# Half of the weight remainders of a two-block transformer: a DMA that adds, in place of GpSimd's subtract

## The chip, the cores and the metric

The kernel runs on one core of one Trainium2 chip, as one launch. The metric is the device time of the launch in microseconds (us), lower is better.

## What is computed

A residual stream of 512 tokens with 1024 features, all in float32, goes through two blocks.

```
def first_block(x, ...):
    for layer in range(2):
        u = rmsnorm(h, norm_mix[layer])
        mix = hgrn2_mixer(u, ...) if layer == 0 else dilated_attention_mixer(u, ...)
        h = h + mix
        h = h + swiglu_ffn(rmsnorm(h, norm_ffn[layer]), ffn_w_in[layer], ffn_w_down[layer])
    return rmsnorm(h, final_norm)

def second_block(x, ...):
    proj = rmsnorm_2(x, norm_mix) @ w_in
    ...
    x = x + (gate_a * (o_a @ w_up_nsa) + gate_b * (o_b @ w_up_gla)) @ w_out
    x = x + (silu(h @ w_ffn_gate) * (h @ w_ffn_up)) @ w_ffn_down
    return rmsnorm_2(x, norm_final)
```

HGRN2 is a linear attention with a forget factor for each feature (8 heads of 128). The dilated attention has 12 heads of 128 in three groups. In the second block `o_a` is a native sparse attention (8 heads of 64 with a compressed, a selected and a window branch) and `o_b` a gated linear attention (4 heads). The feed-forwards have 2816 hidden features. Nearly all of the arithmetic is in products of the 512 tokens with weight matrices.

## The kernel before

**Products.** TensorE (PE) reads operands of the type float32r. Each operand x is split into a head, x cast to float32r, and a remainder (rest), x minus head. `mm3` (line 387) makes a product of three matmuls: rest by head, head by head, head by rest. A feature-major product takes 128 weight columns at a time: one weight block of 128 x 128 against 512 tokens is three matmuls.

**Weights.** `Weights` (line 240) streams the weights in the order of use. The blocks of a section (`hgrn`, the feed-forwards, `attn`, `blk2`) are packed into units of up to 1024 columns, 512 KB; there are 346 units, numbered u = 0 to 345. The first eight are of 512 columns. A unit goes three ways:

- `load`: SP issues the DMA from HBM into `w_raw` (three buffers).
- `heads`: ScalarE (ACT) casts `w_raw` to the head `w_hi`.
- `rests`: VectorE (DVE) for even u, GpSimd (POOL) for odd u, subtracts `w_hi` from `w_raw` into `w_lo`. A pair of `w_hi` and `w_lo` is a split block; there are three.

`take` hands the blocks of a unit to PE, and calls the others as it goes:

```
        if self.idx == 3 * len(widths) // 8:
            self.heads(self.look)
        if self.idx == 5 * len(widths) // 8:
            self.rests()
```

So after 3/8 of unit `at` the heads up to unit `at + look - 1` are put on ACT's queue, after 5/8 the rests on DVE's and GpSimd's. `look` is 1 at first and becomes `SPLIT` in `hgrn` when x[5] has been split (line 807). A unit of a feed-forward is 8 blocks, 24 matmuls.

**Order.** Each engine runs its instructions in the order in which the program lays them out. The mixers are generators, whose steps the program puts between weight products (`tick`, `step`). When a step comes is decided by `Clock` (line 163), a rough model of the four engines with a cost for each instruction issued through the wrappers `v`, `a`, `g` and `t`; a step waits until its inputs should be there. DMAs are no part of that model. The steps' instructions, such as the queries `Q` of HGRN's blocks, `GQ` and `GK` of the gated linear attention, `Pc` of the compressed branch and `P` of attention, are mostly on DVE, and PE then multiplies what they wrote. GpSimd makes, beside the rests, products such as `Q`, `KT`, `T`, `rot`, `rs`, `sg` and the sums of squares `sq_acc`.

At the start the first value products of HGRN take one x tile at a time (`first`, line 802): ACT makes the head of u of x[k], then its square, with the heads of the weights between them, and PE multiplies x[k] with unit k, 12 matmuls.

Nearly every row of the profile has the line L228, that of the recording helper; tiles tell the instructions apart.

Of the kernel before, what the change touches and what calls it, by code (L numbers as in the profile page):

```python
# [22 lines left out]
UNIT = 1024  # L23

# columns of the packed per-feature vectors
# [10 lines left out]
# columns of the constants that stay  # L36
# [9 lines left out]
# the pairs of heads before which HGRN's value products for heads 0..3 and 4..7 come  # L46
HGRN_V = {0: 0, 2: 1}
# attention's sections: the queries and keys of a head of each group, the values of a group's heads
# [4 lines left out]
def nsa_rows():  # L53
    """Feature order of the NSA heads: tile j holds head j of group 0 and head j of group 1."""
    return np.concatenate([np.arange((e * 4 + j) * 64, (e * 4 + j) * 64 + 64) for j in range(4) for e in range(2)])


def attn_heads():
    """(head of the group, group) in the order in which the output projection takes them."""
    return [(t, g) for t in range(4) for g in (1, 2)] + [(t, 0) for t in range(4)]  # L60


def weight_plan():
    """The order in which weight blocks are used: (section, [(matrix, k tile, columns)])."""
# [74 lines left out]
def plan_units(sec, chunks):  # L139
    """Cut a section's blocks into units of at most UNIT columns; the first ones are small, to start early."""  # L140
    units, cur, w = [], [], 0
    for i, ch in enumerate(chunks):
        n = len(ch[2])
        if w + n > UNIT or (sec == "hgrn" and w and i <= KD):
            units.append((cur, w))
            cur, w = [], 0
        cur.append(ch)
        w += n
    if cur:
        units.append((cur, w))  # L150
    return units
# [11 lines left out]
class Clock:  # L163
    """Rough times of the engines' queues and of the tiles' contents while the program is laid out:
    they say when a background step's inputs and banks will be there, so that TensorE isn't made to wait."""

    def __init__(self, hop):
        self.hop = hop  # from an instruction's end to the start of another engine's that waits for it
        self.free = {"pe": 0.0, "v": 0.0, "a": 0.0, "g": 0.0}
        self.written, self.read = {}, {}  # L170
        self.held = []
# [4 lines left out]
    def banks(self, now):  # L176
        """PSUM banks that are free by then."""
        def free(x):
            r, w = self.read.get(x, (-1.0, "")), self.written.get(x, (0.0, ""))
            return w[0] <= r[0] <= now - self.hop  # L180
        self.held = [x for x in self.held if not free(x)]
        return 8 - len(self.held)
# [57 lines left out]
class Weights:  # L240
    """Streams the weights in the order of use and splits each into its float32r head and rest."""

    RAW, SPLIT = 3, 3
# [18 lines left out]
    def heads(self, look):  # L262
        while self.n_head < min(self.at + look, len(self.units)):
# [5 lines left out]
            self.a.copy(hi[:, :w], self.raw[u][:, :w])  # L269
            self.split[u] = (hi, lo)  # L270
            self.n_head += 1

    def rests(self):
        while self.n_rest < self.n_head:
            u = self.n_rest
            w = self.units[u][2]
            hi, lo = self.split[u]
            (self.g if u % 2 else self.v).tensor_sub(lo[:, :w], self.raw.pop(u)[:, :w], hi[:, :w].bitcast(F32))
            self.n_rest += 1
        self.load(self.n_rest + self.RAW - 1)  # L280
# [31 lines left out]
class Program:  # L312
# [74 lines left out]
    def mm3(self, out, a, b, first, last):  # L387
        """out += a^T b for operands given as (head, rest)."""
# [18 lines left out]
    def gemm(self, xs, M, evac, lead=1, ms=None):  # L407
        """Feature-major product: evac(m, [128 features, 512 tokens]) for each output tile m.
        An operand may be a pair of functions: whether it is there, and what makes it."""
# [13 lines left out]
    def gemm_tok(self, n, residue=False, before=None, after=None, every=1):  # L423
        """Token-major product with n weight columns: four banks of 128 tokens, by blocks or by the rest of the token mod 4."""
# [24 lines left out]
    def norm_feed(self, k, squares=True):  # L449
        """x[k] is final: build the operand's parts and add its squares."""  # L450
# [25 lines left out]
    def sums(self, out, acc, residue=False):  # L476
        """Each token's sum over the partitions of acc, onto the token's partition."""
# [33 lines left out]
    def bcast(self, col, ps=None):  # L511
        """[128 tokens, n] to the first 128 n columns of a PSUM bank that hold every token's value on all partitions."""
# [50 lines left out]
    #  # L563
    # A head's score of query t and key s <= t is q_t . (forget factors of s+1..t) k_s. Keys and queries meet
    # block by block: when neighbouring blocks of h tokens are joined, the queries carry the factors from their
    # block's start, the keys those to their block's end and T holds each block's product, so that every factor
    # is a product of forget factors and nothing is divided.
# [5 lines left out]
    def decay4(self, Q, K, T, have, Vj, done):  # L573
        """Two heads whose values are there when have() says so, with keys K[e] [128, 512] and forget
        factors T [128, 2, 512]; Q[e] [128, 2, 512] holds head e's queries and,
        beside them, room. Blocks are joined four at a time: the room takes the queries that reach back further
        than the block before theirs, with the factors of the blocks between.
        Vj(e, j) gives head e's values of tokens 128 j.. as [tokens, 128]; done(e, o) takes the normed output,
        not yet times its gain."""
        v, a, g = self.v, self.a, self.g  # L580
        # per level: each block's product, and the products of the blocks after each of the first three
# [25 lines left out]
        def begin(e, h, T):  # L607
            """The room's queries for blocks of h tokens."""
# [57 lines left out]
    def decay2(self, Q, K, T, Vj, done):  # L666
        """Two heads on one set of keys K and forget factors T [128, 1, 512], whose queries Q [128, 2, 512] are
        zero outside each head's features. Blocks are joined two at a time."""
# [39 lines left out]
    def decay_out(self, Q, K, T, Sd, have, Vj, done):  # L708
        """Sd holds the scores within each block of 128 tokens. The blocks before come through a state
        [features, values] that is carried from block to block."""  # L710
# [49 lines left out]
    def hgrn(self):  # L760
# [16 lines left out]
        # TensorE's clock is released by activity: these run while the first operands are on their way  # L777
# [99 lines left out]
    def attn(self):  # L877
# [13 lines left out]
        def scores(gi, q, k, st):  # L891
            """Masked scores and their exponentials of one head, four blocks of 128 queries."""
# [27 lines left out]
        def merge(hg, st):  # L920
            """Softmax over the three groups' log-sum-exps, then the weighted outputs."""
# [109 lines left out]
    def block2(self):  # L1031
# [28 lines left out]
        # compressed keys and values  # L1060
# [30 lines left out]
        # gated linear attention operands  # L1091
# [25 lines left out]
        # token-major columns  # L1117
# [62 lines left out]
        # sparse attention  # L1180
# [4 lines left out]
        def rope(raw, i):  # L1185
            """Rotate, then stack the parts of the 64 features for products in two passes: q as head on one
            half of the partitions and rest on the other, k's head on both halves and k's rest on both."""
# [92 lines left out]
        def w_stage(j, e, br, P, l):  # L1280
            """Softmax's sum and the branch's gate, onto the rows of P."""
# [5 lines left out]
        def pt_stage(P):  # L1287
            """P transposed to keys x queries, in parts: [(key block, head, rest)] with columns of queries from there on."""
# [16 lines left out]
        def pv_stage(j, e, br, PT):  # L1305
            """Value products; the values' heads go to rows 0..63 and their rests to rows 64..127."""
# [150 lines left out]
    def finish(self, hh):  # L1457
        """The last output tile in two halves of the tokens, so that the first half is normed and stored under the second."""
# [29 lines left out]
        def store(p, factors, k):  # L1488
            """Feature tiles k and k + 1."""
# [68 lines left out]
def levels():  # L1558
    """Where a key (row) and a query (column) meet as blocks are joined: two at a time, for blocks of 1..32 tokens
    and the second blocks' queries; then four at a time, for blocks of 1, 4 and 16, with the queries of the last  # L1560
    three blocks against the block before theirs, of the last two against the first and of the last against the second."""
# [11 lines left out]
def rope_tables():  # L1573
    """cos, and the sine with the sign that the other half takes; both [128 dims, 512 tokens]."""
# [6 lines left out]
def rope2_tables():  # L1581
    """Tables of the partial rotation for two stacked heads of 64, and the swap of its two halves."""
# [12 lines left out]
def feat(a):  # L1595
    """A vector over features as [128, tiles]."""
    return np.asarray(a, np.float32).reshape(-1, 128).T
# [54 lines left out]
```

## Time and profile before

| what | value |
|---|---|
| median of 3 runs | 2163.91 us (2163.86 to 2165.43) |
| span of the profiled execution, first to last instruction | 2162.1 us |
| difference of the two | 1.8 us |
| matmuls | 9983 |
| granted clock of PE, mean | 0.994 |
| HBM read | 187.25 MB |

The profiled execution is known by its span; its time as a run is not given apart, so 1.8 us beside the span stand for what lies around it. A row of a timeline gives the start and the length in us, the engine, the operation with output and inputs, and in brackets for how long the engine stood idle before it and what released it. PE is the matmul side of TensorE, PEld its weight loads.

### The profile page before, as it was taken

What the parts mean: (1) busy time and instruction counts of PE and PEld (TensorE: products, weight loads), DVE (VectorE), ACT (ScalarE), POOL (GpSimd) and SP (SyncE); (2) the same over time, 40 slices, a digit from 0 to 9 for tenths busy, and PEclk for the clock granted to TensorE, in tenths of its full rate; (3) what the DMA queues carried; (4) which work ended last, traced back from release to release, by engine and by line L of the source; (5) the groups of instructions that cost most, each with busy time, mean ns of one, the idle gap of its engine ahead of it and who ended that gap; (6) DMA issues with size and microseconds to landing.
All of it is one profiled execution on the core that took longest, in us unless ns stands there. A gap on an engine that the chain in (4) does not pass through costs nothing.

```text
span 2162.1 us, 25412 instructions
## 1 busy us (share of the span) xinstructions
PE 2117.4 (98%) x9983; PEld 1773.4 (82%) x9983; DVE 1004.3 (46%) x1775; ACT 783.8 (36%) x1290; POOL 723.6 (33%) x442
## 2 busy tenths in 40 slices
PE   9999999999999999999999999999899999999998
PEld 7787788888888998788888888887688788888887
DVE  4778853322334555643322333447778753222322
ACT  5343443222233433443222224244455543222233
POOL 4413343323333434323322335331511253322333
PEclk9999999999999999999999999999999999999999
DMA  5111233323323222222332232321111223333332
GB/s 178 59 59 49 69 127 98 98 98 98 98 88 107 79 88 78 79 69 98 98 102 93 98 98 92 133 69 48 55 55 57 70 95 98 98 98 98 96 100 69
DMA packets 55865, 191.00 MB, mean 88 GB/s; under 512 B 6257, under 2 KB 8321, under 8 KB 55745
## 3 DMA queue, kind: packets, MB, share of 16 engines
q1 hardware_dynamic: 53584, 183.85, 26.2%
q0 software_dynamic: 1008, 3.42, 0.4%
q10 hardware_dynamic: 1152, 2.10, 0.3%
q8 instruction: 78, 1.28, 0.2%
q14 instruction: 43, 0.34, 0.1%
HBM read 187.25 MB, written 2.10 MB: 88 GB/s over the span
## 4 chain that ended last, share of the span: by engine, by line
PE 86%; DVE 9%; issue 1%; POOL 1%; ACT 1%; DMA 1%; SPq 0%; DVEq 0%; ACTq 0%; POOLq 0%
PE ps L228 86%; DVE Q L228 2%; DVE Sd L228 2%; DVE P L228 1%; DMA w_raw<-in_hgrn 1%; DVE w_lo L228 1%; DVE K L228 0%; POOL rot L228 0%; DVE Pc L228 0%; DVE qs L228 0%; POOL rs L228 0%; DVE obl L228 0%; DVE GQ L228 0%; DVE PT L228 0%; POOL w_lo L228 0%
## 5 line engine op out<-in xcount | busy, mean ns | idle before, releaser
L228 PE MATMUL ps<-u,w_hi 128*128 128x512 f32 x3392 | 1049.4, 391 | 0.0
L228 PEld LDWEIGHTS ps<-u,w_hi 128*128 128x128 f32 x3392 | 638.9, 188 | 128.9 <-issue 1.4
L228 PE MATMUL ps<-u,w_lo 128*128 128x512 f32 x1696 | 683.7, 403 | 2.2 <-POOL w_lo L228 2.2
L228 POOL TENSOR_TENSOR w_lo<-w_raw,w_hi 128x1024 fp32r<-128x1024 f32 (+2 forms) x173 | 415.8, 2403 | 745.1 <-ACT w_hi L228 636.2
L228 ACT CAST w_hi<-w_raw 128x1024 fp32r<-128x1024 f32 (+2 forms) x346 | 356.1, 1030 | 301.6 <-PE ps L228 205.4
L228 PEld LDWEIGHTS ps<-u,w_lo 128*128 128x128 f32 x1696 | 319.7, 189 | 68.3 <-issue 4.2
L228 PE MATMUL ps<-h,w_hi 128*128 128x512 f32 (+1 forms) x1078 | 326.3, 385 | 0.0
L228 DVE TENSOR_TENSOR w_lo<-w_raw,w_hi 128x1024 fp32r<-128x1024 f32 (+2 forms) x173 | 231.5, 1338 | 183.7 <-ACT w_hi L228 175.4
L228 PEld LDWEIGHTS ps<-h,w_hi 128*128 128x128 f32 x1078 | 200.9, 188 | 40.4
L228 PE MATMUL ps<-h,w_lo 128*128 128x512 f32 (+1 forms) x539 | 207.6, 385 | 0.5 <-DVE x L228 0.5
L228 POOL TENSOR_TENSOR sg<-sg,r_bc 128x512 f32<-128x512 f32 x66 | 85.8, 1299 | 290.3 <-ACT sg L228 290.3
L228 DVE TENSOR_TENSOR x<-x,ps 128x512 f32<-128x512 f32 (+1 forms) x73 | 49.5, 678 | 218.6 <-PE ps L228 218.6
L228 PE MATMUL ps<-w_hi,u 128*128 128x512 f32 (+1 forms) x448 | 139.1, 392 | 2.3 <-DVE u L228 2.3
L228 DVE TENSOR_TENSOR h<-ps,sg 128x512 f32<-128x512 f32 x66 | 45.7, 692 | 194.9 <-PE ps L228 182.4
L228 ACT ACTIVATE sg<-gs 128x512 f32<-128x512 f32 x66 | 41.7, 632 | 242.3 <-DVE gs L228 242.3
L228 ACT CAST h<-h 128x512 fp32r<-128x512 f32 x66 | 41.0, 620 | 242.8 <-DVE h L228 242.8
L228 DVE TENSOR_TENSOR gs<-ps,r_bc 128x512 f32<-128x512 f32 x66 | 45.6, 691 | 156.8 <-PE ps L228 156.7
L228 PEld LDWEIGHTS ps<-h,w_lo 128*128 128x128 f32 x539 | 101.2, 188 | 20.9 <-DVE x L228 0.7
L228 ACT ACTIVATE P<-P,nm 128x128 f32<-128x128 f32 (+2 forms) x112 | 55.2, 494 | 142.6 <-DVE nm L228 130.4
L228 POOL TENSOR_TENSOR sq_acc<-sq_acc,sq 128x512 f32<-128x512 f32 x48 | 67.2, 1405 | 117.8 <-ACT sq L228 115.7
L228 PEld LDWEIGHTS ps<-w_hi,u 128*128 128x128 f32 x448 | 95.0, 226 | 10.3 <-DVE u L228 2.7
L228 PE MATMUL ps<-w_lo,u 128*128 128x512 f32 (+1 forms) x224 | 85.8, 383 | 0.0
(294 smaller groups left out, 2231.5 us busy)
## 6 DMA issues: line engine op xcount, KB each, us to landing
w_raw<-in_ffn SPq DMA_DIRECT2D x198, 512.0 KB, 3.5
w_raw<-in_attn SPq DMA_DIRECT2D x48, 512.0 KB, 3.5
w_raw<-in_blk SPq DMA_DIRECT2D x47, 512.0 KB, 3.4
w_raw<-in_hgrn SPq DMA_DIRECT2D x36, 512.0 KB, 3.5
w_raw<-in_blk SPq DMA_DIRECT2D x7, 404.0 KB, 2.9
x<-in_xt SPq DMA_DIRECT2D x8, 256.0 KB, 5.1
w_raw<-in_hgrn SPq DMA_DIRECT2D x8, 256.0 KB, 4.0
x<-in_xt ACTq DMA_DIRECT2D x8, 256.0 KB, 5.0
```

Source lines behind the costliest of these rows:

```text
L228: r = f(*args, **kw)
```

## The change

From unit 9 on, an odd unit's remainder is no longer a subtract on GpSimd. ACT writes the head, as before, and then the negative of the head into `w_lo`. GpSimd then issues a DMA that reads the weights from HBM a second time and adds them to what stands in `w_lo`. Even units keep their subtract on DVE, and units 1, 3, 5 and 7 theirs on GpSimd. Four split blocks are held instead of three, and with them `look` becomes 4. The scratch space for GpSimd's DMA descriptors, `dynamic_dma_scratch_size`, is set to 4096. Comments and docstrings are left out as well, which the diff below doesn't show.

```diff
-    RAW, SPLIT = 3, 3
+    RAW, SPLIT, DIRECT = 3, 4, 8
...
             self.a.copy(hi[:, :w], self.raw[u][:, :w])
+            if u >= self.DIRECT and u % 2:
+                self.a.activation(lo[:, :w], hi[:, :w].bitcast(F32), AF.Copy, scale=-1.0)
             self.split[u] = (hi, lo)
...
-            w = self.units[u][2]
+            ap, _, w = self.units[u]
             hi, lo = self.split[u]
-            (self.g if u % 2 else self.v).tensor_sub(lo[:, :w], self.raw.pop(u)[:, :w], hi[:, :w].bitcast(F32))
+            raw = self.raw.pop(u)
+            if u < self.DIRECT or u % 2 == 0:
+                (self.g if u % 2 else self.v).tensor_sub(lo[:, :w], raw[:, :w], hi[:, :w].bitcast(F32))
+            else:
+                self.nc.gpsimd.dma_start(lo[:, :w], ap, accum_op=ALU.add)
...
-    nc = bacc.Bacc("TRN2", target_bir_lowering=False, num_devices=1)
+    nc = bacc.Bacc("TRN2", target_bir_lowering=False, num_devices=1, dynamic_dma_scratch_size=4096)
```

The first place is ACT's queue at the start of the program. `x_96`, `x_98` and `x_100` are x[5], x[6] and x[7]; the two casts of 128x512 are units 6 and 7, the casts of 128x1024 units 8, 9 and, in the second fence, 10. Before:

```order
L228 CAST w_hi_258<-w_raw_232 128x512
L228 CAST w_hi_261<-w_raw_256 128x512
L228 ACTIVATE sq_270<-x_96 128x512
L228 ACTIVATE u_285<-x_98,vec_78 128x512
L228 CAST w_hi_288<-w_raw_266 128x1024
L228 ACTIVATE sq_294<-x_98 128x512
L228 ACTIVATE u_309<-x_100,vec_78 128x512
```

After the change:

```order
L228 CAST w_hi_258<-w_raw_232 128x512
L228 CAST w_hi_261<-w_raw_256 128x512
L228 CAST w_hi_266<-w_raw_264 128x1024
L228 ACTIVATE sq_276<-x_96 128x512
L228 ACTIVATE u_291<-x_98,vec_78 128x512
L228 CAST w_hi_294<-w_raw_272 128x1024
L228 ACTIVATE w_lo_295<-w_hi_294 128x1024
L228 ACTIVATE sq_301<-x_98 128x512
L228 ACTIVATE u_316<-x_100,vec_78 128x512
```

The cast of unit 8 has moved ahead of the square of x[5] and of u of x[6], the cast of unit 9 ahead of u of x[7], with the new negation behind it.

The second place is GpSimd's queue in block 2, where the gated linear attention begins and the rotations (`rot`) of the sparse attention's keys and queries stand. Before:

```order
L228 TENSOR_TENSOR rot<-kraw,tab 128x512
L228 TENSOR_TENSOR rot<-rot,rot_10466 128x512
L228 TENSOR_TENSOR w_lo<-w_raw,w_hi 128x1024 x3
L228 TENSOR_TENSOR rot<-kraw,tab 128x512
L228 TENSOR_TENSOR rot<-rot,rot_10881 128x512
L228 TENSOR_TENSOR rot<-qraw,tab 128x512
L228 TENSOR_TENSOR rot<-rot,rot_10916 128x512
L228 TENSOR_TENSOR rs<-rs,rsg 128x512
```

After the change:

```order
L228 TENSOR_TENSOR rot<-kraw,tab 128x512
L228 TENSOR_TENSOR rot<-rot,rot_10589 128x512
L285 DMA w_lo<-in_blk 128x1024 x2
L228 TENSOR_TENSOR rot<-kraw,tab 128x512
L228 TENSOR_TENSOR rot<-rot,rot_11006 128x512
L228 TENSOR_TENSOR rot<-qraw,tab 128x512
L228 TENSOR_TENSOR rot<-rot,rot_11041 128x512
L285 DMA w_lo<-in_blk 128x1024
L228 TENSOR_TENSOR rs<-rs,rsg 128x512
L228 TENSOR_TENSOR rs<-go,rs 128x512
```

Where three subtracts stood between the two keys' rotations there are now two DMAs, and the third comes after the first query's; the other instructions keep their order.

## Rows read from the trace of the kernel before

**Rows 1.** Section 1 of the page: busy us, share of the span, instructions of each engine.

```profile
PE 2117.4 (98%) x9983; PEld 1773.4 (82%) x9983; DVE 1004.3 (46%) x1775; ACT 783.8 (36%) x1290; POOL 723.6 (33%) x442
```

**Rows 2.** Windows: length; PE, PEld, DVE, ACT, POOL busy us (instructions); PEclk, DMA share, GB/s.

```profile
55.00:320.00 265.00, 250.44 (x1310) 211.08 (x1309) 196.38 (x392) 107.35 (x214) 88.98 (x77) 0.99 0.21 72
320.00:620.00 300.00, 300.00 (x1329) 248.29 (x1328) 90.82 (x106) 84.33 (x103) 93.21 (x50) 1.00 0.30 98
1310.00:1800.00 490.00, 473.58 (x2383) 396.64 (x2382) 308.98 (x598) 224.15 (x431) 170.00 (x115) 0.99 0.23 75
```

**Rows 3.** PE's waits: for what; us in total, times, longest us.

```profile
PE ps L228 <- DVE Q L228: 10.4, 9, 2.1
PE ps L228 <- DVE GK L228: 6.6, 3, 3.0
...
PE ps L228 <- POOL w_lo L228: 2.2, 1, 2.2
PE ps L228 <- DVE Pc L228: 1.9, 2, 1.3
PE ps L228 <- DVE P L228: 1.8, 3, 1.3
```

**Rows 4.** Timeline in HGRN: start us, us, engine, line, operation, count, idle before.

```profile
170.02 2.01 DVE L228 TENSOR_TENSOR Q<-Q,F 128x128 f32<-128x128 f32 x4
...
175.97 3.82 DVE L228 TENSOR_TENSOR Q<-Q,F 128x128 f32<-128x128 f32 x2
...
176.96 2.55 POOL L228 TENSOR_TENSOR w_lo<-w_raw,w_hi 128x1024 fp32r<-128x1024 f32 x1
```

**Rows 5.** Timeline in the gated linear attention of block 2.

```profile
1455.48 2.52 POOL L228 TENSOR_TENSOR w_lo<-w_raw,w_hi 128x1024 fp32r<-128x1024 f32 x1
1455.83 2.45 DVE L228 TENSOR_TENSOR GK<-GK,GF 128x256 f32<-128x256 f32 x1
...
1460.22 0.42 DVE L228 TENSOR_TENSOR GK<-GK,T 128x256 f32<-128x256 f32 x1
```

**Rows 6.** Windows around three pauses, columns as in rows 2.

```profile
181.00:185.00 4.00, 3.94 (x12) 3.64 (x13) 3.83 (x12) 0.00 (x0) 0.00 (x0) 0.57 0.31 117
1457.00:1465.00 8.00, 6.57 (x26) 5.98 (x27) 7.88 (x11) 0.22 (x1) 1.00 (x1) 0.57 0.33 99
1549.50:1553.50 4.00, 3.64 (x11) 2.78 (x12) 3.90 (x6) 2.34 (x4) 2.24 (x3) 0.57 0.39 131
```

**Rows 7.** Section 5 of the page: GpSimd's remainders; busy us, mean ns, idle us before.

```profile
L228 POOL TENSOR_TENSOR w_lo<-w_raw,w_hi 128x1024 fp32r<-128x1024 f32 (+2 forms) x173 | 415.8, 2403 | 745.1 <-ACT w_hi L228 636.2
```

**Rows 8.** Windows of instructions on w_lo alone; columns as in rows 2, without ACT.

```profile
55.00:320.00 265.00, 109.06 (x258) 48.56 (x257) 21.23 (x16) 39.74 (x17) 0.99 0.21 72
...
1310.00:1800.00 490.00, 213.61 (x526) 99.44 (x525) 44.46 (x33) 78.43 (x33) 0.99 0.23 75
```

**Rows 9.** Timeline of ACT in the second feed-forward.

```profile
1249.80 0.62 ACT L228 CAST h<-h 128x512 fp32r<-128x512 f32 x1 [3.94 <-DVE h L228]
1250.33 1.05 ACT L228 CAST w_hi<-w_raw 128x1024 fp32r<-128x1024 f32 x1
```

**Rows 10.** Timeline: GpSimd issues four DMAs, DVE beside it.

```profile
1354.96 2.12 POOL L1057 DMA_DIRECT2D w<-in_w  x4
...
1355.92 1.22 DVE L228 TENSOR_TENSOR w_lo<-w_raw,w_hi 128x1024 fp32r<-128x1024 f32 x1
```

**Rows 11.** DMA view: issues, KB each, median us to landing.

```profile
w_raw<-in_ffn SPq DMA_DIRECT2D x198, 512.0 KB, 3.5
...
w<-in_w POOLq DMA_DIRECT2D x4, 512.0 KB, 7.9
```

**Rows 12.** Timeline of ACT at the start, and PE's pause.

```profile
21.05 0.71 ACT L228 ACTIVATE u<-x,vec 128x512 fp32r<-128x512 f32 x1
23.92 1.05 ACT L228 CAST w_hi<-w_raw 128x1024 fp32r<-128x1024 f32 x1 [2.16 <-DMA w_raw<-in_hgrn]
...
27.97 1.22 PE L228 MATMUL ps<-w_hi,u 128*128 128x512 f32 x2 [2.32 <-DVE u L228]
```

## The prediction

> **What bounds the kernel now.** I read the page's busy shares first, then a table of windows by stage, then the list of PE's waits, then single pauses in the timeline. PE is busy for 2117.4 of 2162.1 us [rows 1], so no change outside PE can save more than the 44.7 us that are left, plus what the clock loses. The windows show where these are [rows 2]: a feed-forward stretch has none (300.00 of 300.00 us busy, 1329 matmuls, 0.226 us each), the HGRN stretch from 55 to 320 us has 14.6, the stretch from 1310 to 1800 us (end of the second feed-forward, then block 2) has 16.4. The list of PE's waits says for what [rows 3]: tiles of DVE above all. Only 2.2 us are a wait for a weight remainder.
>
> The reader is to see why DVE is late there. At 176.96 us GpSimd starts a remainder of 2.55 us [rows 4]. The two DVE products that begin at 175.97 take 3.82 us together, although four of the same shape took 2.01 us in all at 170.02. PE, which reads them, stands for 2.1 us, its longest wait for Q [rows 3]. At 1455.48 us the same [rows 5]: a remainder of 2.52 us on GpSimd, a DVE product of 2.45 us (another of 128 x 256 takes 0.42 us at 1460.22), and PE's longest wait for GK, 3.0 us [rows 3]. A DVE product with both inputs in SBUF and a GpSimd remainder do not run side by side here. The longer one holds the other up by about its own length. A pause costs twice: around three of them the granted clock is at 0.57 in windows of 4, 8 and 4 us [rows 6], that is, at 1.2 instead of 2.4 GHz for most of them. The work lost is 16 us x 0.43 = 6.9 us.
>
> **The change part by part.** Units 9, 11, ... 345 make 169 of GpSimd's 173 remainders.
>
> *Removed: 169 subtracts on GpSimd*, 2.40 us each [rows 7]. GpSimd itself is not the bound; what counts is DVE behind it. The waits in which I found or expect such a product are those for Q, GK, Pc and P, and the one for w_lo: 10.4 + 6.6 + 1.9 + 1.8 + 2.2 = 22.9 us [rows 3]. Not all of it goes, since other GpSimd products stand there too (Q, KT, T, rot, rs). Remainders are 39.74 of 88.98 us of GpSimd's time in HGRN and 78.43 of 170.00 in block 2 [rows 2, 8], 46% together: 10.5 us is the low end, 22.9 the high one. I take two thirds, 15.3 us, since a remainder stands in both of the pauses traced. Of the clock's 6.9 us I take two thirds too, 4.6 us (ends 0 and 6.9).
>
> *Added: 169 negations on ACT* of 128 x 1024, priced as the cast of that shape, 1.05 us [rows 9]: 177 us, so ACT goes from 783.8 us, 36% [rows 1], to 961 us, 44%. In the feed-forwards each has room: ACT stands idle for 3.94 us before the cast of h that precedes a head [rows 9]. In HGRN and block 2 a negation can stand ahead of something that PE waits for. I take 4 us for this and for pauses that the new order of the steps makes. The ends are 0 and 15, the second nearly what those two stretches lose today. On PE the steps move most in HGRN and in the sparse attention; those of the gated linear attention keep their places (second order fence: its neighbours on GpSimd).
>
> *Added: 169 DMAs from GpSimd's queue.* An issue costs it 0.53 us: the four of 512 KB issued at 1354.96 took 2.12 us [rows 10]. That is less than the subtract that goes, so what stands behind it on GpSimd (sg, sq_acc, Q, KT) starts earlier. No row shows an accumulating DMA. The nearest: a plain 512 KB load on SP's queue lands 3.5 us after issue, and those four on GpSimd's in 7.9 us [rows 11]. The low end is 3.5. As the adding one reads its destination too, twice 7.9 = 15.8 is the high end. I take 7.9, the row with the same queue and size.
>
> How late may it land? Heads are made when 3/8 of a unit is used, now for the third unit ahead instead of the second. In a feed-forward a unit is 24 matmuls, 5.42 us, so from there to the first use are 2 5/8 units = 14.2 us. The cast and the negation take 2 x 1.05 us off it, 12.1 us are left. With 7.9 us the DMA has 4 us to spare, and the feed-forwards, 198 units [rows 11] or 1073 us, cost nothing and gain nothing. If that cover is gone, PE waits for w_lo. The added loads are half of what SP's queue moves, and there the DMA engines are busy for 0.30 of their time [rows 2]. Even counted twice the new ones make it 0.60, and the raw blocks are fetched ahead.
>
> The Trainium skill speaks against this part ("SBUF — State Buffer", section "SBUF: two separate sides"): descriptors of a DMA that GpSimd issues cannot be written while DVE holds the port pair that both share, so such a DMA waits for DVE. The trace does not show it at the issue: the four took 0.53 us each beside a DVE remainder of 1.22 us [rows 10]. By the rule a landing would come up to 1.22 us later, at 9.1 us, and the sum would stay; it makes the late landings below a little likelier.
>
> *Moved: the first heads.* The cast of unit 8 now stands ahead of u of x[6], and cast and negation of unit 9 ahead of u of x[7] (first order fence). The cast of unit 8 waits for its load until 23.92 us [rows 12], so u of x[6], made at 21.05 us before, comes after it, at 25 us or later. PE then stands one x tile earlier: it pauses before the 12 matmuls of x[6] instead of those of x[7], and starts them no sooner than the 27.97 us at which it now starts the others, since the same chain (that cast, a square and u on ACT, u on DVE) then stands ahead of them. That is 12 x 0.226 = 2.7 us later. The ends are 0 and 5 (5 if x[7], behind one more cast and negation, is late as well).
>
> Sum: -15.3 - 4.6 + 4 + 2.7 = -13.2 us. The profiled execution has a span of 2162.1 us. The median of the three runs shown is 2163.91, so 1.8 us lie around the span. Against the median: 2163.9 - 13.2 = 2150.7, and I say **2151 us**. This case's own range is 2141 to 2159.
>
> **The rivals.** *A new order, the same pauses.* GpSimd keeps its other products, ACT has 177 us more, and the planner, which knows nothing of GpSimd's DMAs or of DVE being held up, lays out HGRN and the sparse attention anew. For it: more than half of GpSimd's time in the stretches with pauses is not remainders [rows 2, 8]. Against it: the two pauses traced stand behind remainders. Taking the low ends (-10.5, clock 0) and the high end of 15 for ACT with 2.7 at the start, 2163.9 - 10.5 + 15 + 2.7 = 2171; taking 6 for ACT, 2162. I put it at 2158 to 2170, centre 2163.
>
> *The DMAs land late: slower.* Place: PE's wait for w_lo at the first use of an odd unit. It decides from a landing of 12.1 us after issue on. A pause s at each odd unit also lengthens the lead of the next by s, so a landing of L gives s = (L - 12.1) / 2. Each us beyond costs 169 x 0.5 = 85 us: at 13.1 us the time is about 2236, at the high end of 15.8 us 2163.9 - 13.2 + 3.7 x 85 = 2465. For it: no row has such a DMA. Against: 4 us to spare. The Trainium skill's rule above would act here.
>
> *Late in a few places only.* Block 2 and the edges of stages have less lead: PE waits 2.2 us for a remainder once today [rows 3]. Ten such places of 2 us against the gain of 13 make 2171.
>
> **How the numbers follow.** Forecast 0.62, new order 0.20, late everywhere 0.10, late in places 0.08. A measurement of this kernel can tell about 0.2%, 4.3 us, from no change. The forecast lies wholly below 2159.6; of the new order a third does, two thirds are within 0.2%: faster 0.69, same 0.13, slower 0.18. The range of 2140 to 2170 takes in the forecast, the new order and leaves out the late landings and a little of what lies below.
>
> **What would show it.** GpSimd's busy time falls by about 400 us, to 320, and DVE's by some 40 to 60. PE's waits for Q, GK, Pc and P fall from 20.7 us to under 10. The clock is full at 1457 to 1465 us, and GK there takes under 0.8 us. The new DMAs land in 6 to 10 us, and PE stays at 300 us of 300 in the feed-forward. The start is 2 to 3 us longer. Wrong would be: waits for w_lo of more than 10 us in all, or DVE products of 2.4 us still beside GpSimd's DMAs.

## The result and the profile after

The changed kernel takes 2193.68 us (median of 4 runs, 2190.31 to 2195.01), the kernel before 2164.43 us on the same chip: ratio 1.0134, 95% interval 1.0119 to 1.0148. It is slower by 29 us where 13 less were forecast. The profiled execution has a span of 2192.3 us, 30.2 more than before.

The page of the changed kernel: busy time of each engine, two DMA queues, two new groups of instructions and the landing of the new DMAs.

```profile
PE 2129.4 (97%) x9983; PEld 1779.7 (81%) x9983; DVE 943.0 (43%) x1775; ACT 969.3 (44%) x1464; POOL 444.6 (20%) x442
...
q1 hardware_dynamic: 53584, 183.85, 26.1%
q0 software_dynamic: 25344, 91.60, 25.2%
...
L228 ACT ACTIVATE w_lo<-w_hi 128x1024 fp32r<-128x1024 f32 (+3 forms) x169 | 178.5, 1056 | 5.3
L285 POOL DMA_DIRECT2D w_lo<-in_ffn x99 | 86.7, 875 | 447.0 <-ACT w_lo L228 447.0
...
w_lo<-in_ffn POOLq DMA_DIRECT2D x99, 512.0 KB, 5.8
```

Against [rows 1], VectorE has lost 61 us and GpSimd 279; ScalarE has gained 186. The parts do what they were meant to do. PE, however, is busy for 12.0 us more with the same 9983 matmuls, and span less busy time has gone from 44.7 to 62.9 us. So 18.2 us are new pauses and 12.0 us are matmuls at the lower clock: 30.2 together.

The windows say where. Of the changed kernel:

```profile
55.00:320.00 265.00, 252.22 (x1314) 211.23 (x1313) 173.88 (x392) 125.18 (x232) 61.09 (x76) 0.99 0.41 104
320.00:620.00 300.00, 300.00 (x1329) 248.39 (x1328) 90.67 (x106) 112.19 (x130) 52.46 (x50) 1.00 0.60 145
...
1700.00:1770.00 70.00, 51.56 (x227) 41.87 (x227) 39.66 (x105) 35.80 (x71) 9.61 (x8) 0.83 0.20 49
```

And the last of these stretches in the kernel before:

```profile
1700.00:1770.00 70.00, 67.72 (x310) 55.59 (x309) 43.73 (x58) 35.56 (x50) 28.79 (x15) 1.00 0.26 83
```

The feed-forward is full as before [rows 2], so the DMAs hold PE up nowhere in this stretch. HGRN has 12.8 us of pauses in place of 14.6. From 1700 to 1770 us PE stands for 18.4 us where it stood for 2.3, at a granted clock of 0.83 in place of 1.00, and does 227 matmuls instead of 310. That is the end of the sparse attention.

PE's waits of the changed kernel (us in total, times, longest us), against [rows 3]:

```profile
PE ps L228 <- ACT oan L228: 12.3, 3, 4.9
PE ps L228 <- DVE Q L228: 8.6, 10, 1.8
PE ps L228 <- DVE GK L228: 6.9, 7, 1.9
PE ps L228 <- DVE P L228: 5.8, 4, 2.5
PE ps L228 <- DVE u L228: 5.3, 1, 5.3
PE ps L228 <- DMA w_lo<-in_blk: 3.5, 1, 3.5
```

The first is new in this size (before, PE waited for `oan` once, for 1.0 us): `oan` are the sparse attention's normed outputs, the operand of the product with `w_up_nsa`, which the expectations below call upn. The timeline of PE at this product, in the changed kernel (start us, us, what, in brackets the idle time before it):

```profile
1715.33 0.80 PE L228 MATMUL ps<-oan,w_lo 128*128 128x512 f32 x1 [3.93 <-ACT oan L228]
...
1721.84 1.38 PE L228 MATMUL ps<-PT,VV 128*128 128x512 f32 x8
1728.16 0.80 PE L228 MATMUL ps<-oan,w_lo 128*128 128x512 f32 x1 [4.94 <-ACT oan L228]
...
1734.53 1.43 PE L228 MATMUL ps<-PT,VV 128*128 128x512 f32 x8
1737.64 1.29 PE L228 MATMUL ps<-cst,P 128*128 128x128 f32 x10 [1.68 <-DVE P L228]
...
1740.19 1.43 PE L228 MATMUL ps<-PT,VV 128*128 128x512 f32 x8
1744.13 2.37 PE L228 MATMUL ps<-cst,P 128*128 128x128 f32 x10 [2.50 <-DVE P L228]
1746.15 2.09 PE L228 MATMUL ps<-PT,VV 128*128 128x512 f32 x8
1749.26 1.31 PE L228 MATMUL ps<-cst,P 128*128 128x128 f32 x10 [1.02 <-DVE P L228]
...
1751.32 1.49 PE L228 MATMUL ps<-PT,VV 128*128 128x512 f32 x7 [0.22 <-DVE PT L228]
1756.25 0.79 PE L228 MATMUL ps<-oan,w_lo 128*128 128x512 f32 x1 [3.44 <-ACT oan L228]
```

Before, the last value product (`PT,VV`) had ended 6.7 us ahead of the first product with `oan`:

```profile
1714.66 1.37 PE L228 MATMUL ps<-PT,VV 128*128 128x512 f32 x8
...
1722.75 0.39 PE L228 MATMUL ps<-oan,w_lo 128*128 128x512 f32 x1
```

A job of the sparse attention (one head pair's branch) goes through scores (`ks,qs` on PE), softmax (ScalarE, VectorE), transposes (`cst,P`) and the value product. In the changed kernel five value products are still to come when `oan` is asked for. From there to the last of them PE has no weight products but some of those with `oan`, and none at all from 1734.5 to 1756.2 us. So it stands between the steps of one job, and the granted clock falls: `oan` by `w_lo` takes 0.80 us where it took 0.39.

Position by position, I took the time at which PE first reads the remainder of a unit, less the same time before:

| run | unit 12 (start) | unit 44 (HGRN done) | unit 240 (block 2 begun) | unit 280 (block 2 done) |
|---|---|---|---|---|
| changed kernel | +4.1 | +3.2 | +2.6 | +30.1 |
| h: order before, DMAs, four blocks | +2.3 | -9.9 | -10.6 | -19.7 |
| m: order before, subtracts, four blocks | +0.8 | +1.2 | +2.1 | -2.5 |
| f: changed order, subtracts | +3.4 | +22.3 | +21.9 | +52.1 |
| a: heads earlier, subtracts | +4.1 | +20.3 | +19.9 | +33.8 |
| d: order of a, DMAs | +4.5 | +6.0 | +5.2 | +17.0 |
| i: heads as before, new charges, DMAs | +0.1 | -13.0 | -13.4 | -5.0 |
| k: changed order to unit 224, then before's, DMAs | +3.8 | +3.6 | +2.9 | -6.2 |
| e: order before, DMAs, three blocks | +0.4 | -5.3 | +23.1 | +23.0 |

The other lines are the experiments of the next section. From unit 240 to 280, the sparse attention of block 2, the changed kernel loses 27.5 us against before, nearly all of its loss.

### The profile page after: what moved, and what is told of

Same layout as the page of the kernel before. It is cut to its first block, busy times and chain, and to the rows that moved or that the text cites. A ratio compares the mean times of both kernels' runs of the same rounds, so it can differ in the third digit from the quotient of the medians.

```text
span 2192.3 us, 25689 instructions
## 1 busy us (share of the span) xinstructions
PE 2129.4 (97%) x9983; PEld 1779.7 (81%) x9983; DVE 943.0 (43%) x1775; ACT 969.3 (44%) x1464; POOL 444.6 (20%) x442
## 3 DMA queue, kind: packets, MB, share of 16 engines
q1 hardware_dynamic: 53584, 183.85, 26.1%
q0 software_dynamic: 25344, 91.60, 25.2%
## 5 line engine op out<-in xcount | busy, mean ns | idle before, releaser
L228 ACT ACTIVATE w_lo<-w_hi 128x1024 fp32r<-128x1024 f32 (+3 forms) x169 | 178.5, 1056 | 5.3
L285 POOL DMA_DIRECT2D w_lo<-in_ffn x99 | 86.7, 875 | 447.0 <-ACT w_lo L228 447.0
L228 PEld LDWEIGHTS ps<-h,w_lo 128*128 128x128 f32 x539 | 101.2, 188 | 20.9 <-DVE x L228 0.7
```

Of the source, the lines that this page charges most:

```text
L228: r = f(*args, **kw)
L285: self.nc.gpsimd.dma_start(lo[:, :w], ap, accum_op=ALU.add)
```

## The experiments

The question is whether the loss belongs to what the engines now do (negations, adding DMAs) or to the order in which the planner lays it out. The planner's `Clock` charges an engine for what goes through the wrappers. The change touches its books in three ways: heads come a unit earlier, GpSimd is no longer charged for the remainders, and ScalarE is charged for the negations. So order and hardware can be had apart. (The theories and rivals that the expectations number are their own, not those of the prediction.) TensorE's order is, instruction for instruction, that of before in the runs h, m, e and h2, and that of the changed kernel in f.

**Before's order, the change's way with the weights (h).** The books are kept at the old moments, with the old charges; the instructions are issued by the raw engines at the change's moments from unit 8 on.

```diff
     def heads(self, look):
-        while self.n_head < min(self.at + look, len(self.units)):
...
+        while self.p_head < min(self.at + look, len(self.units)):
+            self.p_head += 1
+            self.put_heads(self.p_head)
+            raw, hi, lo = self.aps[self.p_head - 1]
+            self.prog.clock.issue("a", "copy", [hi], [raw])
+        if self.at >= self.DIRECT:
+            self.put_heads(self.at + self.SPLIT)
...
+            self.prog.clock.issue("g" if self.p_rest % 2 else "v", "tensor_tensor", [lo], [raw, hi])
...
-                self.W.look = self.W.SPLIT
+                self.W.look = 3
```

`put_heads` casts and negates on `nc.scalar`; its counterpart `put_rests` subtracts on `nc.vector` and issues the DMA, as in the changed kernel.

> The weights by the change's way (negation on ScalarE, adding DMA, four blocks, heads a unit earlier), but laid out by the books of the kernel before, so that TensorE's order is that of before, instruction for instruction. Theory 1 (the loss is the new layout: five jobs of the sparse attention are left for the products upn and run there one after the other): no loss is left and the gain comes out, 2145 to 2156 us, the waits for oan at the end of the sparse attention under 2 us in all, start-up as before. Rival 2 (ScalarE's 178 us of negations make the chain of the sparse attention late in any order): 2180 us or more, with waits for ScalarE's results at upn as in the changed kernel. Rival 3 (the adding DMAs are late or disturb other transfers): 2170 us or more, waits for w_lo spread over the program.

Measured: 2143.7 us (2142.22 to 2144.25) against 2164.07, ratio 0.9906 (0.9889 to 0.9922). The page of this run, some of its waits, and three windows. The last value product ends at 1696.7 us in this run, so the end of the sparse attention lies in the second:

```profile
PE 2110.5 (99%) x9983; PEld 1770.1 (83%) x9983; DVE 944.3 (44%) x1775; ACT 961.4 (45%) x1459; POOL 446.2 (21%) x442
```

```profile
PE ps L228 <- DVE GK L228: 6.9, 7, 1.9
...
PE ps L228 <- DVE Q L228: 3.7, 2, 3.0
...
PE ps L228 <- DVE oan L228: 1.0, 1, 1.0
```

```profile
55.00:320.00 265.00, 260.82 (x1364) 221.65 (x1363) 180.20 (x396) 130.73 (x236) 63.43 (x77) 0.99 0.44 112
...
1680.00:1750.00 70.00, 68.56 (x316) 56.65 (x315) 38.95 (x59) 43.15 (x60) 17.58 (x15) 1.00 0.56 131
...
1700.00:1770.00 70.00, 69.00 (x305) 56.84 (x304) 35.89 (x45) 34.34 (x46) 21.71 (x19) 1.00 0.61 141
```

ScalarE has the same negations and GpSimd the same DMAs as in the changed kernel, and PE waits for `oan` for 1.0 us. Theory 1 holds; rivals 2 and 3 fall. The order alone is worth 2193.7 - 2143.7 = 50 us. By the table 13.1 us of it are there at unit 44 and 36.6 come from unit 240 to 280. In the HGRN stretch h has pauses of 4.2 us, the changed kernel of 12.8, with ten waits for `Q` (8.6 us) where h has two (3.7). Why the new order makes `Q` late there was not traced.

**The changed order with the old subtracts (f).** The negation is charged but not issued, and GpSimd subtracts, uncharged.

```diff
-                self.a.activation(lo[:, :w], hi[:, :w].bitcast(F32), AF.Copy, scale=-1.0)
+                self.prog.clock.issue("a", "activation", [lo[:, :w]], [hi[:, :w]])
...
-                self.nc.gpsimd.dma_start(lo[:, :w], ap, accum_op=ALU.add)
+                self.nc.gpsimd.tensor_sub(lo[:, :w], raw[:, :w], hi[:, :w].bitcast(F32))
```

> The order of the changed kernel on TensorE, VectorE and GpSimd, instruction for instruction, with four blocks, but GpSimd subtracts as before and ScalarE has no negations. Theory 1 (layout): as slow as the changed kernel or slower, 2190 to 2215 us, with the waits for oan at upn of 10 us or more. Rivals 2 and 3 (ScalarE's load, the DMAs): neither is there, so about the time of before, 2160 to 2172 us.

Measured: 2214.2 us (2212.34 to 2215.79), ratio 1.0234 (1.0218 to 1.0249). Waits of this run:

```profile
PE ps L228 <- DVE Q L228: 16.8, 8, 3.5
PE ps L228 <- ACT oan L228: 10.5, 3, 6.0
PE ps L228 <- DVE P L228: 8.0, 4, 2.8
```

There is no negation and no adding DMA here, and the wait for `oan` is there all the same. The order is slow by itself, and with the subtracts it costs HGRN too (+22.3 at unit 44).

**Before's order with four blocks and subtracts (m).** As h, without the negation, and with `nc.gpsimd.tensor_sub` where the DMA stood.

> The run with before's order, four blocks and the heads from unit 8 on a unit earlier, but GpSimd subtracts as before: no negations and no DMAs. VectorE's order is that of the run with the DMAs, instruction for instruction. It tells how much of that run's gain of 20 us comes from GpSimd leaving VectorE alone, and how much from the earlier heads and the fourth block. Theory 1 (VectorE held up by GpSimd's remainders): 2160 to 2168 us, VectorE busy about 1000 us and waits for Q and GK of 15 us or more as before. Rival 5 (the earlier heads did it): 2143 to 2150 us.

Measured: 2161.57 us (2161.21 to 2163.49), ratio 0.9993 (0.9984 to 1.0003): no difference from before. Page and waits:

```profile
PE 2117.5 (98%) x9983; PEld 1775.5 (82%) x9983; DVE 995.4 (46%) x1775; ACT 783.9 (36%) x1290; POOL 709.7 (33%) x442
```

```profile
PE ps L228 <- DVE Q L228: 11.0, 4, 5.1
PE ps L228 <- DVE GK L228: 6.5, 4, 3.8
```

So earlier heads and a fourth block give nothing by themselves, and rival 5 falls. Between m and h PE's and VectorE's orders are the same; GpSimd's subtracts are replaced by negations and DMAs. VectorE does the same 1775 instructions in 944.3 instead of 995.4 us, the pauses (span less PE's busy time) go from 2159.5 - 2117.5 = 42.0 to 2142.2 - 2110.5 = 31.7, and PE's busy time falls by 7.0 us with the clock: 17.3 us, the whole difference of the spans.

**The earlier heads in the books (a).** The changed kernel with `DIRECT = 1000`: every odd unit is subtracted by GpSimd, and charged.

> Four blocks and the heads a unit earlier alone; GpSimd subtracts all odd units and the planner charges it for them. The layout is then about half as bad as the changed kernel's: two jobs of the sparse attention are left among the products of upn, where the changed kernel leaves five. Theory 1: 2168 to 2185 us, with waits for oan or its makers at upn of 3 to 10 us. Rivals 2 and 3: about 2160 to 2168 us, as neither negations nor adding DMAs are there.

Measured: 2196.93 us (2195.2 to 2201.03), ratio 1.0157 (1.0142 to 1.0172), more than expected: the end of the sparse attention costs 13.9 us (from unit 240 to 280), as expected, but HGRN loses 20 us besides, with 17.1 us of waits for `Q`. That I had not foreseen. In this order three value products follow the first product with `oan`; the expectation, which spoke of two jobs, counted their transposes.

**The same order with the DMAs (d).** The changed kernel, where GpSimd is charged for a subtract beside each DMA.

```diff
                 self.nc.gpsimd.dma_start(lo[:, :w], ap, accum_op=ALU.add)
+                self.prog.clock.issue("g", "tensor_tensor", [lo[:, :w]], [raw[:, :w], hi[:, :w]])
```

(The negation is not charged in this run.)

> The changed kernel, but the planner charges GpSimd for a subtraction where the DMA is issued, so the order is that of the run with four blocks and subtractions, instruction for instruction: two jobs of the sparse attention are left among the products of upn in place of five. Theory 1 (jobs left over cost the time): about half of the changed kernel's loss there: 2172 to 2182 us, waits for oan at upn 3 to 10 us. If the missing charge has nothing to do with it: 2190 us or more.

Measured: 2180.47 us (2179.99 to 2181.75), ratio 1.0082 (1.0067 to 1.0097).

**The missing charge without the earlier heads (i).** As h, but the books have no charge on GpSimd from unit 9 on, and one for the negation. (So the two charges are not told apart.)

> Four blocks, negations and DMAs issued as early as in the changed kernel, but the planner's books keep the heads at three units ahead, and GpSimd is charged nothing, as in the changed kernel: the missing charge alone in the order. Two jobs of the sparse attention are left among the products of upn, a little less tightly than with the earlier heads alone. Theory 1: 8 to 14 us lost there and the start as before: 2155 to 2170 us. If the earlier heads alone make the loss: 2146 us or less.

Measured: 2158.79 us (2157.16 to 2160.88), ratio 0.9979 (0.9969 to 0.9988). Two value products follow the first product with `oan`. PE's waits for it, in d:

```profile
PE ps L228 <- ACT oan L228: 10.9, 2, 7.5
```

and in i:

```profile
PE ps L228 <- ACT oan L228: 9.2, 2, 5.9
```

From unit 240 to 280 h gains 9.1 us. Against that d is 20.9 us behind, i 17.5, the changed kernel 36.6. The earlier heads and the new charges do about half of this harm each, and the value products left over go with it: 3, 2 and 5. With the subtracts the same orders cost nearly as much there: against m, a is 18.5 us behind and f 34.8. In HGRN it is the earlier heads that cost: to unit 44, d is 15.9 us behind h, i is 3.1 ahead.

**The order changed back for block 2 alone (k).** The books go the change's way to unit 223 and before's way from there on; TensorE's order is the changed kernel's in the first part and before's in the second.

> The changed kernel's order up to the second block's mixer (TensorE's order there is that of the changed kernel, instruction for instruction), and from there the order of before; hardware as in the changed kernel throughout. Theory 1 (the layout, and its loss in the sparse attention): the changed kernel stands 2.6 us behind before at the start of the mixer, and before's order with the DMAs won 9 us from there on; so 2164 + 2.6 - 9 = 2158 us, 2153 to 2163, with no wait for oan over 1.5 us. Rival 4 (the order loses in the HGRN stage or by the start-up, and the end of the sparse attention only shows it): 2180 us or more.

Measured: 2157.76 us (2155.57 to 2158.2), ratio 0.9974 (0.9965 to 0.9984), as worked out beforehand. Rival 4 falls: the 36 us between this run and the changed kernel are made in block 2. The 14 us by which it is slower than h are there when block 2 begins (+2.9 against -10.6): they are the changed order's price up to there.

**Three blocks (e).** Before's order, negations and DMAs, `SPLIT = 3`, with the charges of before.

> The order of before, negations and adding DMAs, but three blocks and the heads as late as before. Theory 1: the layout's loss is gone, but a DMA has about 7 us from its issue to the first use in the feed-forward against a landing of 5.8 us, so some wait there: 2148 to 2185 us, with waits for w_lo of up to 0.5 us per odd unit. Rival 2 (ScalarE's load): 2180 us or more with waits for oan. Rival 3 (the DMAs): well over 2185 us.

Measured: 2199.74 us (2195.53 to 2202.21), ratio 1.0165 (1.0150 to 1.0180), 15 us above the highest value expected. The waits of this run:

```profile
PE ps L228 <- DMA w_lo<-in_ffn: 17.2, 9, 4.2
PE ps L228 <- DMA w_lo<-in_blk: 10.2, 3, 5.3
...
PE ps L228 <- DMA w_lo<-in_hgrn: 4.7, 3, 2.7
PE ps L228 <- DMA w_lo<-in_attn: 4.4, 3, 1.9
```

They are few and long (18 of them, 36.5 us), not 0.5 us at each odd unit as I had written. The fourth block, and the earlier heads that it allows, are what the DMAs need: with them h has no such wait.

**The fourth block's head from unit 14 on (h2).** As h, with `if self.at >= 14`.

> Before's order with the DMAs and four blocks, with the fourth block's head from unit 14 on in place of unit 8, so that the cast and the negation of units 10 and 11 do not stand ahead of the first operands on ScalarE. If these casts cost the 2.3 us by which the run with the heads from unit 8 on stood behind before at unit 9: 2141 to 2142 us. If not: 2143.5 us, the same.

Measured: 2142.97 us (2142.83 to 2144.2), ratio 0.9910 (0.9893 to 0.9926). At unit 12 it stands 1.3 us ahead of before where h was 2.3 behind, and at unit 280 1.2 us of that are left. But i, whose engines run the same instructions in the same order as h's up to unit 12, stands 0.1 us behind there, and the medians of h and h2 cannot be told apart. So it is not shown that the casts cost anything at the start. Both are faster than either kernel, by 0.9% against before and by 2.3% against the changed one (2143.7 / 2193.7).

## Why the prediction was wrong

**The gain was there, and its sum had the size given.** Forecast were -15.3 us for VectorE no longer held up and -4.6 for the clock, 19.9 together. Run h against before: pauses 44.7 to 31.7, that is 13.0 us less, and PE busy 6.9 us less, 19.9 in the span. That the sums agree so closely is luck: the first term was 2.3 us too large, the second 2.3 too small. Of the 22.9 us of waits from which the 15.3 were taken, h keeps 11.3 (6.9 for `GK`, 3.7 for `Q`, 0.7 for the others). The waits for `K` are gone as well, and they were not on my list; of before:

```profile
PE ps L228 <- DVE K L228: 3.8, 4, 1.3
```

The second term rested on three pauses [rows 6]. In h the granted clock is full around the products of the two in block 2, but HGRN has another stretch at half clock, behind a wait of 3.0 us for `Q`. One part of the first term was wrong: the 6.6 us for `GK` [rows 3] did not go (6.9 in h and in the changed kernel). In the changed kernel VectorE's `GQ` products there stand beside GpSimd's rotations, which stay. VectorE's timeline:

```profile
1458.31 2.25 DVE L228 TENSOR_TENSOR GQ<-GQ,GF 64x256 f32<-64x256 f32 x2
1460.60 0.42 DVE L228 TENSOR_TENSOR GK<-GK,GF 128x256 f32<-128x256 f32 x1
...
1462.04 0.91 DVE L228 TENSOR_TENSOR GQ<-GQ,T 64x256 f32<-64x256 f32 x2
```

GpSimd's:

```profile
1457.59 1.29 POOL L228 TENSOR_TENSOR rot<-kraw,tab 128x512 f32<-128x512 f32 x1
1458.95 1.33 POOL L228 TENSOR_TENSOR rot<-rot,rot 128x512 f32<-128x512 f32 x1
```

The two `GQ` at 1462.04 have no rotation beside them. The longest wait for `GK` fell from 3.0 to 1.9 us, and the half clock of [rows 6] is gone from there:

```profile
1456.00:1464.00 8.00, 4.55 (x28) 3.27 (x27) 7.81 (x13) 0.00 (x0) 4.70 (x8) 1.00 0.68 175
```

**The step that failed** is the term of +4 us, with ends 0 and 15, "for this and for pauses that the new order of the steps makes". The negations, 178.5 us on ScalarE, cost next to nothing: PE's waits for results of ScalarE are 1.9 us in all in h (1.3 for `ao`, as before, and 0.6 for `sq`). The order cost 50.0 us with the DMAs (changed kernel against h) and 52.6 with the subtracts (f against m). I took the upper end from the pauses that the two stretches had, and misread even these: each has about 15 us [rows 2], the two together 31.0. But a new order is not bounded by the pauses of the old one at all: it can leave work without cover that was covered before. I had seen that "the steps move most in HGRN and in the sparse attention", and compared neighbours in the gated linear attention, where they did not move. Counting the value products behind the first use of `oan` in the new order (five; none before) would have shown the place. What the new order does in HGRN, 13 of the 50 us, stays open.

**The rival of the new order** named the planner's new layout and had 20% of the chance, but was priced at 2158 to 2170 from that same end of 15. It needed a price well above no change.

**The start**: forecast 2.7 us (0 to 5), measured 4.1 at unit 12 in the changed kernel. The mechanism was right: one pause of 5.3 us for u, with 12 matmuls fewer done than at the 2.3 us of [rows 12], ends at 28.02 us. What I left out is the clock: in the first 55 us it is granted at 0.94, before at 0.97, which is 1.7 us more lost.

**The DMAs**: forecast to land in 7.9 us, with 12.1 us before the first use; they land in 5.8 (median), and the feed-forward stays at 300 of 300 us. The late landings did not come, but for one wait of 3.5 us in block 2. There ScalarE made the negation late, so the DMA was issued only at 1561.17 us and landed at 1567.44, just before PE went on. In h, PE waits for no DMA. GpSimd is busy for 444.6 us and not for some 320, because that figure left out the issues themselves: 169 of 0.53 us are 90, and they are recorded with 0.875. In the changed kernel three of the plain issues of [rows 10] are recorded with 0.84 to 0.86 too, though the next one starts 0.5 to 0.6 us after each of the first two; so how long an issue holds GpSimd is not shown.

**The other signs.** PE's waits for Q, GK, Pc and P were to fall from 20.7 us to under 10: they are 24.5 in the changed kernel, which spoke against the forecast at once, and 11.0 in h. `GK` at the place of [rows 5] takes 0.42 us at full clock, as said.

**The rule on the port pair** (the Trainium skill, "SBUF — State Buffer", section "SBUF: two separate sides", on descriptors that GpSimd cannot write until VectorE releases the shared port): the trace shows no such delay here. The median landing is 5.9 us in block 2, where VectorE is busy for 192.75 of 330 us (1500 to 1830), and 5.8 in the feed-forward, where it is busy for 90.67 of 300. Of the 169 adding DMAs, the 48 issued while VectorE was at work landed in 5.7 us, the other 121 in 5.8 (medians). The Trainium skill speaks there of a VectorE instruction in a mode with two ports; no row tells which instructions here run in one, so the 1.22 us that the prediction took from a remainder of VectorE need not follow from it.

## What to carry to other kernels

Where a planner sets the order, an edit changes the planner's books as well as the engines' work, and the two have to be priced apart. Before pricing, lay out the new order and look at each place where a product needs the last result of a background chain: count the chain's steps that are still to come there. If the books are the culprit, keep the old charges for the moved work and issue it beside them: that turned +1.3% into -0.9% here.

## What the runs showed of the hardware

By the times of its packets an adding DMA keeps the DMA engines busy for twice as long as a plain one: queue q0 moved 25344 packets of 91.60 MB, nearly all of them adding, in 25.2% of the engines' time, q1 53584 of 183.85 MB in 26.1%. With 16 engines and a span of 2192.3 us that is 0.35 us a packet against 0.17, with 3.6 and 3.4 KB each. Even so, an adding load of 512 KB lands in 5.8 us. The plain ones on the same queue took 7.9 before the change [rows 11], but these were four in a row, of which the first landed after 6.2 us and the last after 10.0. With DMA engines busy for 0.60 of the time the plain loads of `w_raw` still land in 3.5 us.

What holds VectorE up is GpSimd's computing: VectorE's total fell by 51 us between m and h, though GpSimd's issues are recorded with 148 us in h (169 of 0.875 us). In h 4 of VectorE's own remainders stand beside an issue for more than 0.3 us and take 1.23 us each, as the 111 with nothing beside them do (median); 50 beside GpSimd's computing take 1.58 us on average and up to 2.34.
